# S5 parameter arithmetic on VectorE between the gates of the feed-forward layers, with its transfers queued one at a time

## The chip, the cores and the metric

The kernel runs on one core of a Trainium2 chip. The metric is device microseconds (us) of one execution, as a median of several. TensorE (PE in the profile) multiplies matrices; VectorE (DVE), ScalarE (ACT) and GpSimd (POOL) do elementwise work, each working off its own queue in order. SyncE (SP), ScalarE and GpSimd also issue transfers (DMA), and such an issue stands in the queue of the engine that makes it.

## The reference

One step of a two-layer model of width 1024, for a prompt of 256 tokens and 8 single-token samples (264 columns). Each layer is feed-forward, mixer, feed-forward, each followed by a residual sum and a layer norm. Layer 0 has the even mixer (attention and RWKV-7), layer 1 the odd one (S5). What matters here is the feed-forward and the parameters of S5, which depend on no token:

```
f  = (silu(x @ wg) * (x @ wu)) @ wd               # 1024 -> 2816 -> 1024
x  = layer_norm(alpha * x + 0.5 * f, g, b)

dt  = exp(log_dt)
ar, ai = exp(lr * dt) * cos(li * dt), exp(lr * dt) * sin(li * dt)
cr, ci = ((ar - 1, ai) divided by (lr, li))       # complex
bb  = (cr, ci) * (br, bi)                         # complex, per group, state and channel
s_t = (ar, ai) * s_(t-1) + bb @ u_t               # scan over the tokens
y   = c_re @ sr - c_im @ si + d_skip * u
```

## The kernel before, in words

Tokens lie along the columns, channels on the 128 partitions. Each weight block of 128x128 is loaded in float32, in chunks of 8 blocks (512 KB) on SyncE's queue (`raw`, line 188), and split in two halves: ScalarE casts the high half (`wh`, line 197), VectorE subtracts (`wl`, line 198). A block then takes three matmuls of 264 columns (lines 295 to 297): high by high, high by low, low by high. `Stream.take` starts the splits of the three chunks behind the one in use; four chunks fit.

A feed-forward (`ffn`) has three parts. First the gate blocks m = 0 to 2 are formed from the raw residual sum before its norm is known (`raw`, 48 blocks), while the norm is worked out beside it. Then for m = 3 to 21 there is one gate each: 16 blocks (48 matmuls) into `pg` and `pu`, a Silu on ScalarE (line 458), the product `h` on VectorE (line 460), its high half `hh` on ScalarE (461) and its low half `hl` on VectorE (462). Last come 8 down-projections (`pd`, 22 blocks each), each followed by its part of the residual sum in `put_r`. `stats` ends it: VectorE makes `nmu` (line 389), centres block 0 (line 398) and takes the reciprocal (391); GpSimd centres blocks 1 to 7 in four instructions (line 398 too). VectorE then multiplies each block by `rstd` (line 409), ScalarE scales it (402), and both split it (`xh` 414, `xl` 415). I call the norm at the end of layer 0's mixer the first norm, and that at the end of layer 0's second feed-forward the second norm; the feed-forward behind each begins with raw products.

The S5 parameters are worked out beside the trunk by two Python generators. `s5_first` runs in the first feed-forward: exponentials and sines (on VectorE already), powers of the pole, the zero-order hold, eight readout pieces (a complex product of 64 columns and one of 256), whose results go through TensorE to DRAM (`kd`, `gxd`) 12 pieces later. `s5_second` runs in layer 0's second and layer 1's first feed-forward: powers of the rotation, four rotation tables (`rot`, written to `rotd`), eight products into `FT` (lines 1527 to 1532), and eight pieces that finish the table `T` (1548 to 1551). Each `yield` ends a piece, and `advance` takes one, scheduled behind the last low half `hl`. All of the arithmetic through `tt` and `ts` is on GpSimd. The transfers of `s5_second` are on GpSimd's queue, behind a copy of the first norm's `rstd` (`anchor`).

The order of each engine's queue is set by a scheduler from the traced program; `issue_after` puts an instruction behind another.

Of the kernel before, what the change touches and what calls it, by code (L numbers as in the profile page):

```python
# [30 lines left out]
# pi / 2 and ln 2 in parts of few bits  # L31
# the set of activation tables that has Exp and Ln
# [4 lines left out]
G1 = 3  # L37
CW = 0.5 * math.exp(-0.5)

# blocks of the combined projection  # L40
# [5 lines left out]
# columns of the packed per-channel vectors  # L46
# [5 lines left out]
# columns of the packed constants  # L52
# [107 lines left out]
# accumulators  # L160
# [17 lines left out]
        # what the loads are queued behind  # L178
# [40 lines left out]
class Trunk:  # L219
    def __init__(self, ctx, tc, a, order):  # L220
# [15 lines left out]
        # the pole's fourth power: cosine, sine, magnitude  # L236
# [10 lines left out]
    def load(self):  # L247
        """the tokens, and the operands that are needed later"""
# [23 lines left out]
    def banks(self, **groups):  # L272
        """deals out the groups of accumulators: streams of work that run side by side have their own"""
        self.groups = {tag: list(g) for tag, g in groups.items()}
# [13 lines left out]
    def block(self, ps, key, xh, xl, start, stop, full=False):  # L288
        """three products of halves; the fourth is beneath float32's accuracy"""
# [10 lines left out]
    def behind(self):  # L300
        """what is traced within is queued behind the last block of the trunk's own work"""
# [5 lines left out]
    def advance(self):  # L307
        """a piece of what runs beside the trunk"""
# [4 lines left out]

    def new_r(self, ln, raw=True, tmp=None, pool=False):
        """with raw, the sum's halves are products' operands before its norm is known"""
# [14 lines left out]
    def put_r(self, ln, m, ps, base=None):  # L330
        """a block of the sum. The mean of the first two blocks is taken from all, so that the squares can be summed
        before the last block is there; it lies within two standard deviations of the mean"""
# [42 lines left out]
    def table(self, func, after):  # L375
        """has the table of a function loaded behind an instruction, before the function is needed"""
# [3 lines left out]
    def stats(self):  # L380
        """the norm of the sum"""
# [24 lines left out]
    def unit(self, k):  # L406
        """a block less the mean, over the standard deviation"""
# [18 lines left out]
    def fix(self, ps):  # L426
        """from a product with the raw sum: that with its norm, less a constant, and the constant"""
# [9 lines left out]

    def ffn(self, layer, f, ln_in, ln_out, raw=True):
        nc = self.nc
        with ExitStack() as ctx:  # L440
# [15 lines left out]
            def gate(m, pg, pu):  # L456
# [5 lines left out]
                self.last_v = nc.vector.tensor_tensor(out=hl[:, m, :], in0=h, in1=hh[:, m, :], op=ALU.subtract)  # L462
                return last
# [23 lines left out]
            for m in range(G1, KF):  # L487
# [6 lines left out]
                self.advance()  # L494
                if not raw_in and m < G1 + 5:
# [3 lines left out]
            for m in range(KD):  # L499
# [4 lines left out]
                self.advance()  # L504
# [16 lines left out]
    def slot(self, shape, name, dt=F32):  # L521
        """a tile of up to 4.2 KB a partition"""
        return self.rw.tile(shape, dt, tag="slot", name=name, bufs=11)

    def page(self, shape, name):
        """a tile of up to 2 KB a partition"""
        return self.rw.tile(shape, F32, tag="pg", name=name, bufs=5)

    def tmp(self, shape, name):
        """a tile of up to 1.1 KB a partition"""  # L530
        return self.rw.tile(shape, F32, tag="tmp", name=name, bufs=6)

    def in_proj(self, mb, ps, raw):
        """evacuates a block of the projection; for RWKV's with its token shift"""
# [27 lines left out]
    def _even(self, ctx, ln_in, ln_out):  # L562
# [4 lines left out]
        # small operands  # L567
        # each on its half of the rows
# [28 lines left out]
        # -1e30 where the key is not before the query  # L597
# [84 lines left out]
    def other_half(self, bone, sbb, idb, nmb):  # L682
        """the rest of the input projection, the attention and its half of the output projection, in pieces"""
# [31 lines left out]
    def samples(self, sbb, idx):  # L715
        """both mixers for the samples, in pieces"""
# [5 lines left out]
    def proj(self, mb):  # L722
        """a block of the projection, in pieces"""
# [9 lines left out]
    def load_exp_ln(self):  # L733
        """the table that has both functions"""
# [3 lines left out]
    def rwkv_first(self, lora, hv):  # L738
        """what takes tanh"""
# [18 lines left out]
    def rsqrt(self, o, x):  # L758
        """1 / sqrt(x) by exp and ln, and a step of Newton's; x is lost"""
# [8 lines left out]
    def rwkv_prep(self, hv, bone):  # L768
# [14 lines left out]
        for m in range(4):  # L783
            kr, lw, ti = self.kr_t[:, m, :], self.lw[:, m, :], self.ti[:, m, :]
            # unit key
# [9 lines left out]
            # decay, summed over a chunk  # L795
# [8 lines left out]
            # keys  # L804
# [18 lines left out]
    def rwkv_tokens(self, bone):  # L823
        """what takes the values"""
# [23 lines left out]
    def to_tokens(self, src, dst):  # L848
        """[(h2,j), m, t] to [(h2,t), (m,c), j], in pieces"""
        nc = self.nc  # L850
        d = dst.rearrange("p (m x) j -> p m x j", m=4)
        for m2 in range(2):
# [5 lines left out]
            # rows are (c2, t), columns (h2, j)  # L858
# [7 lines left out]
    def gram(self, x, out, banks):  # L866
        """[(h2,s), (m,c), (A|R) t] of x with A and R, masked, in pieces"""
# [14 lines left out]
    def rwkv_inverse(self):  # L882
# [5 lines left out]
        # inverse of I + L in ever larger diagonal blocks  # L888
# [42 lines left out]
    def rwkv_chain(self, bone):  # L931
        """from chunk to chunk"""
# [55 lines left out]
    def rwkv_gate(self):  # L988
        """gate and bonus with the group norm's factor and constant, in pieces"""
# [9 lines left out]
    def rwkv_out(self, c, bone):  # L999
        """group norm, bonus and gate of a chunk, the last with the samples"""  # L1000
# [14 lines left out]
        # 1 / sqrt by exp and ln, and a step of Newton's  # L1015
# [13 lines left out]
    def split_out(self, src, k0, s):  # L1029
        """the halves of a part of what goes into the output projection"""  # L1030
# [108 lines left out]
    def sample_values(self, idx):  # L1139
# [41 lines left out]
        # rows (g, d), columns (b4, h) to channels (h2, d), columns (m, b)  # L1181
# [5 lines left out]
    def sample_rwkv(self):  # L1187
# [10 lines left out]
        # partitions (half, b, h)  # L1198
# [44 lines left out]

    def complex(self, scr):
        """temporaries, and products of pairs of real and imaginary parts"""
        nc = self.nc
        Q = 32
        tt = nc.gpsimd.tensor_tensor
# [629 lines left out]
```

## Time and profile before

| | |
|---|---|
| three runs | 1212.99, 1215.94, 1216.66 us, median 1215.94 us |
| profiled execution | span 1214.5 us from its first to its last instruction; what lies around the span is not listed for it, and the median is 1.4 us above its span |
| TensorE | busy 1127.3 us, 93% of the span |
| VectorE | busy 848.4 us, 70% |
| ScalarE | busy 577.0 us, 48% |
| GpSimd | busy 451.1 us, 37% |

Busy shares are means over stages with different limits. Where TensorE runs without a pause, work on another engine costs nothing; the stretches where it stops, or runs at a lower granted clock, are those to look at.

### The profile page before, as it was taken

The numbers are of one execution on the slowest core, as the hardware profiler recorded it, in microseconds if no ns is written. First come the engines' busy times: TensorE is split into PE (matmuls) and PEld (weight loads), VectorE is DVE, ScalarE is ACT, GpSimd is POOL, SyncE is SP. The second block draws the span as 40 slices with busy tenths as digits, with TensorE's granted clock in tenths as the row PEclk, the third lists the DMA queues.
The fourth block names the chain that finished last, engine by engine and source line by source line (L and its number), as shares of the span: only waits on it lengthen the run. The fifth ranks groups of instructions, "written<-read, shape, count | busy, mean of one in ns | idle before, by whom it ended". The sixth has DMA issues, their size and how long they took to land.

```text
span 1214.5 us, 26118 instructions
## 1 busy us (share of the span) xinstructions
PE 1127.3 (93%) x10583; PEld 1067.4 (88%) x10583; DVE 848.4 (70%) x1364; ACT 577.0 (48%) x966; POOL 451.1 (37%) x731
## 2 busy tenths in 40 slices
PE   7999999889999998799999869999968999999995
PEld 7999899887986688799998769999957899999994
DVE  4966566989876679656579785555669699655564
ACT  4544544663355565444543354444352257544442
POOL 0399940446344207377799930000034201000001
PEclk9999999989999999899999879999978999999998
DMA  7666565534564334766666436665556253655551
GB/s 246 231 193 199 195 183 179 154 105 129 154 196 129 106 96 146 209 211 213 204 208 192 132 109 189 186 179 187 175 156 201 95 163 124 214 184 184 181 174 36
DMA packets 66122, 204.95 MB, mean 169 GB/s; under 512 B 13465, under 2 KB 16617, under 8 KB 65745
## 3 DMA queue, kind: packets, MB, share of 16 engines
q1 hardware_dynamic: 56400, 174.09, 45.5%
q0 software_dynamic: 6560, 23.27, 6.1%
q10 hardware_dynamic: 3040, 5.92, 1.5%
q8 instruction: 83, 1.36, 0.5%
q14 instruction: 39, 0.31, 0.1%
HBM read 192.22 MB, written 10.86 MB: 167 GB/s over the span
## 4 chain that ended last, share of the span: by engine, by line
PE 56%; POOL 21%; DVE 11%; DMA 6%; ACT 3%; issue 3%; ACTq 0%; SPq 0%; DVEq 0%; POOLq 0%
PE pd L295 5%; PE pd L297 5%; PE pd L296 5%; PE pg L295 4%; PE pg L296 4%; PE pg L297 4%; PE pu L296 3%; PE pu L295 3%; PE pu L297 3%; DVE wl L198 2%; PE pi L295 2%; POOL fv L1269 2%; POOL fu L1268 2%; POOL fu L1272 2%; POOL fv L1273 2%
## 5 line engine op out<-in xcount | busy, mean ns | idle before, releaser
L198 DVE TENSOR_TENSOR wl<-raw,wh 128x1024 fp32r<-128x1024 f32 (+2 forms) x317 | 405.3, 1279 | 213.8 <-ACT wh L197 212.9
L197 ACT CAST wh<-raw 128x1024 fp32r<-128x1024 f32 (+2 forms) x317 | 329.8, 1041 | 397.8 <-issue 173.8
L297 PE MATMUL pd<-hh,wl 128*128 128x264 f32 x704 | 201.1, 286 | 3.5 <-DVE wl L198 3.5
L295 PE MATMUL pd<-hh,wh 128*128 128x264 f32 x704 | 200.3, 285 | 0.0
L296 PE MATMUL pd<-hl,wh 128*128 128x264 f32 x704 | 199.2, 283 | 0.0
L295 PE MATMUL pg<-xh,wh 128*128 128x264 f32 x648 | 186.2, 287 | 6.5 <-ACT wh L197 2.3
L296 PE MATMUL pg<-xl,wh 128*128 128x264 f32 x648 | 184.9, 286 | 5.6 <-DVE xl L415 5.6
L297 PE MATMUL pg<-xh,wl 128*128 128x264 f32 x648 | 184.9, 285 | 0.0
L295 PE MATMUL pu<-xh,wh 128*128 128x264 f32 x608 | 172.6, 284 | 0.0
L296 PE MATMUL pu<-xl,wh 128*128 128x264 f32 x608 | 172.6, 284 | 0.0
L297 PE MATMUL pu<-xh,wl 128*128 128x264 f32 x608 | 172.4, 284 | 0.0
L297 PEld LDWEIGHTS pd<-hh,wl 128*128 128x128 f32 x704 | 132.6, 188 | 4.5 <-DVE wl L198 4.4
L295 PEld LDWEIGHTS pd<-hh,wh 128*128 128x128 f32 x704 | 132.4, 188 | 0.3
L296 PEld LDWEIGHTS pd<-hl,wh 128*128 128x128 f32 x704 | 132.4, 188 | 0.0
L295 PEld LDWEIGHTS pg<-xh,wh 128*128 128x128 f32 x648 | 123.3, 190 | 7.8 <-ACT wh L197 2.5
L296 PEld LDWEIGHTS pg<-xl,wh 128*128 128x128 f32 x648 | 123.5, 191 | 5.8 <-DVE xl L415 5.8
L297 PEld LDWEIGHTS pg<-xh,wl 128*128 128x128 f32 x648 | 122.9, 190 | 0.0
L398 POOL TENSOR_TENSOR r<-r,nmu 128x528 f32<-128x528 f32 (+1 forms) x24 | 31.0, 1320 | 240.8 <-DVE nmu L389 240.8
L296 PEld LDWEIGHTS pu<-xl,wh 128*128 128x128 f32 x608 | 114.9, 189 | 0.0
L295 PEld LDWEIGHTS pu<-xh,wh 128*128 128x128 f32 x608 | 114.7, 189 | 0.0
L297 PEld LDWEIGHTS pu<-xh,wl 128*128 128x128 f32 x608 | 114.3, 188 | 0.0
L1581 POOL MEMSET us<- 128x256 f32 x1 | 0.3, 312 | 177.5 <-PE pd L297 177.5
(509 smaller groups left out, 2423.5 us busy)
## 6 DMA issues: line engine op xcount, KB each, us to landing
raw<-in_w SPq DMA_DIRECT2D x308, 512.0 KB, 4.0
rotd<-T POOLq DMA_DIRECT2D x4, 768.0 KB, 5.5
raw<-in_w SPq DMA_DIRECT2D x7, 384.0 KB, 7.3
gxd<-gc SPq DMA_DIRECT2D x8, 256.0 KB, 2.5
qb<-qd POOLq DMA_DIRECT2D x8, 256.0 KB, 4.1
FT<-wd POOLq DMA_DIRECT2D x8, 256.0 KB, 9.9
bF<-in_bF POOLq DMA_DIRECT2D x8, 256.0 KB, 4.0
rot<-rotd ACTq DMA_DIRECT2D x5, 384.0 KB, 4.6
```

The costliest lines, as they stand in the source:

```text
L197: nc.scalar.copy(wh[:, :w], raw[:, :w])
L198: nc.vector.tensor_tensor(out=wl[:, :w], in0=raw[:, :w], in1=wh[:, :w], op=ALU.subtract)
L295: mm(ps, lhsT=wh, rhs=xh, start=start, stop=False)
L296: mm(ps, lhsT=wh, rhs=xl, start=False, stop=False)
L297: self.last_mm = mm(ps, lhsT=wl, rhs=xh, start=False, stop=stop)
L398: e.tensor_tensor(out=d, in0=d, in1=self.nmu[:, None, :].to_broadcast([128, k1 - k0, NT]), op=ALU.add)
L1268: tt(out=u, in0=x[0], in1=y[0], op=M)
L1269: tt(out=v, in0=x[1], in1=y[1], op=M)
L1272: tt(out=u, in0=x[0], in1=y[1] if im is None else im, op=M)
L1273: tt(out=v, in0=x[1], in1=y[0], op=M)
L1581: nc.gpsimd.memset(us[:, :, :, 0:8], 0.0)
```

## The change

The arithmetic of both generators moves from GpSimd to VectorE (`tt`, `ts`), and the three plain copies (`gx`, the magnitude of `rot`, `T`) to ScalarE. In the feed-forwards that begin with raw products only two gates of three take a piece, and the down-projections none; in the first feed-forward every gate takes one, and the down-projections the rest. `s5_second` no longer hangs its transfers on the first norm: `now()` makes GpSimd copy one column of the latest gate's `h` (`mark`) and puts the transfer behind that copy. `FT`'s eight loads, `bF`'s eight and `T`'s eight are issued one with a piece, `bF` one piece ahead of its use; every second rotation table has a tile of its own. The core of the diff:

```diff
                 self.last_v = nc.vector.tensor_tensor(out=hl[:, m, :], in0=h, in1=hh[:, m, :], op=ALU.subtract)
+                self.mark = h[:, 0:1]
...
                 last = gate(m, pg, pu)
-                self.advance()
-                if not raw_in and m < G1 + 5:
+                if not raw_in or m % 3:
                     self.advance()
...
                 self.last = self.put_r(ln_out, m, ps) + [self.last_mm]
-                self.advance()
+                if first:
+                    self.advance()
...
     def complex(self, scr):
-        tt = nc.gpsimd.tensor_tensor
+        tt = nc.vector.tensor_tensor
...
     def s5_first(self, scr):
-        tt = nc.gpsimd.tensor_tensor
-        ts = nc.gpsimd.tensor_scalar
+        tt = nc.vector.tensor_tensor
+        ts = nc.vector.tensor_scalar
...
-                nc.gpsimd.tensor_copy(gx[:, :, 0, :, 0], cG[:, :, 0])
+                nc.scalar.copy(gx[:, :, 0, :, 0], cG[:, :, 0])
...
     def s5_second(self, pool, scr):
-        tt = nc.gpsimd.tensor_tensor
+        tt = nc.vector.tensor_tensor
...
-        anchor = nc.gpsimd.tensor_copy(us[:, 0, 0], self.rstd[:, :Q])
-        with self.tc.issue_after(anchor.ins):
-            nc.gpsimd.dma_start(out=self.s0, in_=a["s5_in"])
-            nc.gpsimd.dma_start(out=self.as0, in_=self.as0d)
-            nc.gpsimd.dma_start(out=self.sel, in_=a["sel"])
-        for g in range(2):
-            for j in range(4):
-                src = wd[j, g].rearrange("q r p -> (q r p)")[None]
-                with self.tc.issue_after(anchor.ins):
-                    nc.gpsimd.dma_start(out=FT[g * 64 + j:g * 64 + 64:4].rearrange("p q r c -> p (q r c)"),
-                                        in_=src.to_broadcast([16, Q * 128]))
+        seen = scr.tile([128, 1], F32, name="seen")
+        @contextmanager
+        def now():
+            with self.tc.issue_after(nc.gpsimd.tensor_copy(seen, self.mark).ins):
+                yield
+        def loads():
+            for g in range(2):
+                for j in range(4):
+                    src = wd[j, g].rearrange("q r p -> (q r p)")[None]
+                    with now():
+                        nc.gpsimd.dma_start(out=FT[g * 64 + j:g * 64 + 64:4].rearrange("p q r c -> p (q r c)"),
+                                            in_=src.to_broadcast([16, Q * 128]))
+                    yield
...
-            with self.tc.issue_after(anchor.ins):
+            with now():
                 nc.gpsimd.memset(rot[:, :, 0, :, 0:1], 1.0)
                 nc.gpsimd.memset(rot[:, :, 1:3, :, 0:1], 0.0)
-                nc.gpsimd.tensor_copy(rot[:, :, 2, :, 1:64], q4(rho4).to_broadcast([128, SR // 4, 4, 63]))
+            nc.scalar.copy(rot[:, :, 2, :, 1:64], q4(rho4).to_broadcast([128, SR // 4, 4, 63]))
+            next(load)
...
                 if lv == 4:
                     yield
+                    next(load)
...
+        def factors(s):
+            bF = t_([128, SL, 2, 64], "bF", 2)
+            with now():
+                nc.gpsimd.dma_start(out=bF, in_=a["bF"][:, s * SL:s * SL + SL])
+            return bF
+        nc.gpsimd.memset(T, 0.0)
+        bFs = [factors(0)]
+        yield
         for s in range(Q // SL):
...
+            if s + 1 < Q // SL:
+                bFs.append(factors(s + 1))
+            bF = bFs.pop(0)
...
+            with now():
+                g, j = divmod(s, 4)
+                nc.gpsimd.dma_start(out=T[g * 64 + j:g * 64 + 64:4, :, j * 16:64],
+                                    in_=kd[:, g, :, 0:64 - j * 16].rearrange("q c f -> c q f"))
...
-            nc.gpsimd.tensor_copy(T[:, q], u)
+            nc.scalar.copy(T[:, q], u)
```

How this moves the queues is shown at three places. The first is GpSimd's queue (POOL) at the first norm. There L398 is the centring of blocks 1 to 7, and FT is the table that is loaded from `wd`. Before:

```order
L398 TENSOR_TENSOR r<-r,nmu 128x264
L398 TENSOR_TENSOR r<-r,nmu 128x528 x3
L1483 COPY us<-rstd 128x32
L1485 DMA s_6501<-in_s_in 128x512
L1486 DMA as_6502<-as0d 128x512
L1487 DMA sel<-in_sel 128x128
L1492 DMA FT<-wd 16x4096 x8
```

The same place in the changed kernel, where L1488 is the copy in `now()`:

```order
L398 TENSOR_TENSOR r<-r,nmu 128x264
L398 TENSOR_TENSOR r<-r,nmu 128x528 x3
L326 COPY rl<-gbl 128x8x2
L325 COPY rh<-gbh 128x8x2
L1488 COPY seen<-h 128x1
L1517 MEMSET T 128x2x4
L1518 MEMSET T 128x2x8
L1488 COPY seen<-h 128x1
L1496 DMA FT<-wd 16x4096
```

The eleven loads that stood straight behind the centring are gone from there; one load of `FT` stands behind each copy of a gate's `h`. The second place is GpSimd's queue at the second norm; L1548 to L1551 finish a slice of `T`. Before:

```order
L1548 TENSOR_TENSOR fu<-cst,dU 128x256
L1550 TENSOR_TENSOR fu<-fu,T 128x256
L1551 COPY T<-fu 128x256
L398 TENSOR_TENSOR r<-r,nmu 128x264
L398 TENSOR_TENSOR r<-r,nmu 128x528 x3
L326 COPY rl<-gbl 128x8x2
L325 COPY rh<-gbh 128x8x2
```

And in the changed kernel, at the same norm:

```order
L1488 COPY seen<-h 128x1
L1536 DMA bF<-in_bF 128x512
L1488 COPY seen<-h 128x1
L1550 DMA T<-kd 16x32x48
L398 TENSOR_TENSOR r<-r,nmu 128x264
L398 TENSOR_TENSOR r<-r,nmu 128x528 x3
L326 COPY rl<-gbl 128x8x2
L325 COPY rh<-gbh 128x8x2
```

No arithmetic of S5 is ahead of the centring any more; what is ahead of it hangs on a gate (`h`) of the feed-forward whose down-projections come in between. The third place is VectorE's queue (DVE) in the gates of the first feed-forward. Before, from one `h` to the next:

```order
L460 SCALAR_TENSOR_TENSOR h<-sg,pu 128x264
L198 TENSOR_TENSOR wl<-raw,wh 128x1024
L462 TENSOR_TENSOR hl<-h,hh 128x264
L198 TENSOR_TENSOR wl<-raw,wh 128x1024
L460 SCALAR_TENSOR_TENSOR h<-sg,pu 128x264
```

In the changed kernel, a part of a gate that carries a readout piece (`fu`, `fv` and `gx` are its temporaries and results):

```order
L462 TENSOR_TENSOR hl<-h,hh 128x264
L1269 TENSOR_TENSOR fu<-cb,ap 128x256
L1270 TENSOR_TENSOR fv<-cb,ap 128x256
L1416 TENSOR_SCALAR gx_969<-cb 128x4x16
L1271 TENSOR_TENSOR gx_968<-fu,fv 128x4x16x4
L1273 TENSOR_TENSOR fu<-cb,nai 128x256
L1274 TENSOR_TENSOR fv<-cb,ap 128x256
L198 TENSOR_TENSOR wl<-raw,wh 128x1024
L1275 TENSOR_TENSOR gx_968<-fu,fv 128x4x16x4
L460 SCALAR_TENSOR_TENSOR h<-sg,pu 128x264
L1269 TENSOR_TENSOR fu<-W,cb 128x64
L1270 TENSOR_TENSOR fv<-W,cb 128x64
```

Thirteen instructions of the piece now stand between the four of the gate. Over the whole program VectorE's queue grows by some 400 instructions, and GpSimd's shrinks by as many.

## Rows read from the trace of the kernel before

**Rows 1.** The page: span, busy share of each engine, granted clock in 40 slices.

```profile
span 1214.5 us, 26118 instructions
PE 1127.3 (93%) x10583; PEld 1067.4 (88%) x10583; DVE 848.4 (70%) x1364; ACT 577.0 (48%) x966; POOL 451.1 (37%) x731
PEclk9999999989999999899999879999978999999998
```

**Rows 2.** Windows: us, busy (x count) of PE, PEld, DVE, ACT, POOL; clock; DMA; GB/s.

```profile
25.00:50.00 25.00, 24.04 (x199) 23.83 (x198) 22.64 (x78) 14.11 (x23) 3.67 (x9) 1.00 0.71 246
...
212.00:236.00 24.00, 24.00 (x189) 23.61 (x188) 22.41 (x35) 15.29 (x28) 9.23 (x17) 1.00 0.58 177
...
484.00:508.00 24.00, 16.51 (x118) 16.12 (x118) 15.40 (x40) 12.82 (x24) 2.40 (x12) 0.86 0.69 185
...
508.00:608.00 100.00, 100.00 (x830) 100.00 (x830) 60.73 (x70) 48.73 (x72) 78.19 (x164) 1.00 0.67 215
...
644.00:672.00 28.00, 24.97 (x201) 24.33 (x199) 27.86 (x21) 10.00 (x13) 27.40 (x32) 1.00 0.65 200
672.00:724.00 52.00, 35.53 (x231) 33.60 (x231) 38.10 (x60) 23.06 (x37) 33.91 (x39) 0.80 0.37 115
```

**Rows 3.** Waits of TensorE: us in total, times, longest; 470 to 725, then 0 to 230.

```profile
PE raw L297 <- DVE wl L198: 8.9, 1, 8.9
PE pg L296 <- DVE xl L415: 5.6, 1, 5.6
...
PE pg L295 <- DVE fixc L430: 1.9, 1, 1.9
...
PE pk L1445 <- POOL gx L1274: 2.8, 1, 2.8
```

**Rows 4.** Timeline of VectorE and GpSimd at the second norm: start, us, instruction, [idle before].

```profile
685.16 0.42 DVE L389 TENSOR_TENSOR nmu<-nmu,dl 128x264 f32<-128x264 f32 x1
...
702.38 5.09 DVE L409 TENSOR_TENSOR r<-r,rstd 128x264 f32<-128x264 f32 x5 [11.43 <-POOL r L398]
...
701.61 4.88 POOL L398 TENSOR_TENSOR r<-r,nmu 128x264 f32<-128x264 f32 x4
```

**Rows 5.** Behind the first norm: GpSimd's and ScalarE's timeline, transfers of 476 to 496.

```profile
479.79 2.46 POOL L1492 DMA_DIRECT2D FT<-wd  x5
...
494.01 1.05 ACT L197 CAST wh<-raw 128x1024 fp32r<-128x1024 f32 x1 [6.03 <-DMA raw<-in_w]
...
raw<-in_w SPq DMA_DIRECT2D x4, 512.0 KB, 12.6
FT<-wd POOLq DMA_DIRECT2D x8, 256.0 KB, 9.9
```

**Rows 6.** Transfers of 625 to 700: line, count, KB each, median us to landing.

```profile
raw<-in_w SPq DMA_DIRECT2D x18, 512.0 KB, 4.2
bF<-in_bF POOLq DMA_DIRECT2D x6, 256.0 KB, 4.2
```

**Rows 7.** The splits on VectorE, 500 to 600 and 636 to 684: ns minimum/median/maximum.

```profile
L198 DVE TENSOR_TENSOR wl<-raw,wh x36: 1214/1225/1504, 501.0 to 598.4; 128x1024 fp32r<-128x1024 f32 x36
...
L198 DVE TENSOR_TENSOR wl<-raw,wh x14: 1410/1754/2878, 638.4 to 682.0; 128x1024 fp32r<-128x1024 f32 x14
```

**Rows 8.** VectorE's timeline in the first feed-forward, and one strided product by form.

```profile
48.86 0.22 DVE L1307 SCALAR_TENSOR_TENSOR er<-er,ex 128x64 f32<-128x64 f32 x1
49.00 0.43 DVE L462 TENSOR_TENSOR hl<-h,hh 128x264 fp32r<-128x264 f32 x1
49.34 0.22 DVE L1307 SCALAR_TENSOR_TENSOR er<-er,ex 128x64 f32<-128x64 f32 x1
...
57.33 0.23 DVE L1333 SCALAR_TENSOR_TENSOR fu<-fv,fu 128x64 f32<-128x64 f32 x1
57.59 0.23 DVE L1334 SCALAR_TENSOR_TENSOR fv<-fu 128x64 f32<-128x64 f32 x1
...
L1748 DVE TENSOR_TENSOR mix<-t,po x5: 610/617/631, 982.2 to 1004.2; 128x256 f32<-128x256 f32 x5
```

More of the change, by code (lines that the diff above doesn't have):

```diff
@@ L1501, in s5_second @@
         yield
+        load = loads()
         for s in range(Q // SR):
             q = slice(s * SR, s * SR + SR)
-            rot = T.rearrange("p q f -> p (q f)")[:, :SR * 192].rearrange("p (s r q c) -> p s r q c", s=SR // 4, r=3, q=4)
+            if s % 2:
+                rot = scr.tile([128, SR // 4, 3, 4, 64], F32, name="rot", tag="rot", bufs=1)
+            else:
+                rot = T.rearrange("p q f -> p (q f)")[:, :SR * 192].rearrange("p (s r q c) -> p s r q c", s=SR // 4, r=3, q=4)
             q4 = lambda v: v[:, q].rearrange("p (s q) -> p s q", q=4)[:, :, :, None]
-            with self.tc.issue_after(anchor.ins):
+            with now():
                 nc.gpsimd.memset(rot[:, :, 0, :, 0:1], 1.0)
                 nc.gpsimd.memset(rot[:, :, 1:3, :, 0:1], 0.0)
-                nc.gpsimd.tensor_copy(rot[:, :, 2, :, 1:64], q4(rho4).to_broadcast([128, SR // 4, 4, 63]))
+            nc.scalar.copy(rot[:, :, 2, :, 1:64], q4(rho4).to_broadcast([128, SR // 4, 4, 63]))
+            next(load)
             for lv in range(6):
@@ L1517, in s5_second @@
                     yield
+                    next(load)
             nc.gpsimd.dma_start(out=self.rotd[:, s * SR // 4:(s + 1) * SR // 4], in_=rot)
             yield
+        def factors(s):
[6 more added lines that the diff above has]
+        yield
         for s in range(Q // SL):
             q = slice(s * SL, s * SL + SL)
-            bF = t_([128, SL, 2, 64], "bF", 2)
-            with self.tc.issue_after(anchor.ins):
-                nc.gpsimd.dma_start(out=bF, in_=a["bF"][:, q])
+            if s + 1 < Q // SL:
+                bFs.append(factors(s + 1))
+            bF = bFs.pop(0)
             F0, F1, b0, b1 = FT[:, q, 0], FT[:, q, 1], bF[:, :, 0], bF[:, :, 1]
+            with now():
+                g, j = divmod(s, 4)
+                nc.gpsimd.dma_start(out=T[g * 64 + j:g * 64 + 64:4, :, j * 16:64],
+                                    in_=kd[:, g, :, 0:64 - j * 16].rearrange("q c f -> c q f"))
             u, v, x = (t_([128, SL, 64], n) for n in ("fu", "fv", "kt"))
@@ L1533, in s5_second @@
             yield
-        nc.gpsimd.memset(T, 0.0)
-        for g in range(2):
-            for j in range(4):
-                nc.gpsimd.dma_start(out=T[g * 64 + j:g * 64 + 64:4, :, j * 16:64],
-                                    in_=kd[:, g, :, 0:64 - j * 16].rearrange("q c f -> c q f"))
         dU = scr.tile([128, Q], F32, name="dU")
-        with self.tc.issue_after(anchor.ins):
+        with now():
             nc.gpsimd.dma_start(out=dU, in_=a["dU"])
+            nc.gpsimd.dma_start(out=self.s0, in_=a["s5_in"])
+            nc.gpsimd.dma_start(out=self.as0, in_=self.as0d)
+            nc.gpsimd.dma_start(out=self.sel, in_=a["sel"])
         dm = cst[:, C_DM:C_DM + 64]
```

## The prediction, made before the result was known

> **What bounds the kernel now.** I read the page first. TensorE is busy for 93% of the span, so only the stretches where it stops or runs slowly can give anything back; the granted clock is at its upper level in most slices and dips in a few [rows 1]. Windows of 25 us over the whole span, then the waits of TensorE, led to three such stretches that have S5's parameter work in them. The rest of the lost time (the end of the even mixer, the S5 mixer, the very end) has none of it and should stay.
>
> To price a stretch I count matmuls. In 508 to 608 TensorE never stops and starts 830 in 100 us, 0.1205 us each [rows 2].
>
> The worst stretch is the second norm. TensorE started 201 matmuls in 644 to 672 and 231 in 672 to 724 [rows 2], 432 in 80 us where 664 would fit. A norm costs some of that anyway: round the norm of the first feed-forward, where GpSimd has nothing of S5 left, 189 start in 24 us where 199 fit [rows 2], 10 short. That leaves 222 matmuls, 26.7 us. What made them late stands in two places. VectorE has `nmu` at 685.16, but GpSimd begins to centre with it only at 701.61, 16 us later, and VectorE sits idle for 11.43 us until a centred block is there [rows 4]; the splits `wl` that TensorE needs next are queued behind that, and TensorE waits 8.9 us in one piece [rows 3]. In those 16 us GpSimd worked off pieces of S5, the last slices of `T`, that are ahead of the centring in its queue. Its raw products (48 blocks, 144 matmuls, 17.3 us) had covered the norm until about 700, just not long enough. After the stop the clock is at the lower level (1.2 GHz) for a while: the mean over 672 to 724 is 0.80 [rows 2]. Before the norm VectorE is full, 27.86 of 28 us in 644 to 672, and the same split of 128x1024 takes 1754 ns by median against 1225 earlier [rows 2, 7], so that TensorE loses some of its time to late splits even ahead of the norm.
>
> The second stretch follows the first norm. Straight behind the centring GpSimd issues eleven loads, eight of them `FT`, at some 0.5 us each [rows 5]. The four weight chunks issued there take 12.6 us to land, against 4.2 later [rows 5, 6], so ScalarE waits 6.03 us for one [rows 5] with the Silu of the gate behind it, and through `h` and `xl` TensorE waits 5.6 us [rows 3]. In 484 to 508 it starts 118 matmuls where 199 fit: 81 short, 9.8 us, the clock at 0.86 in the mean [rows 2].
>
> The third is small: in the first feed-forward TensorE waits 2.8 us for a readout table `gx` of GpSimd [rows 3].
>
> **The change part by part.** *The centring.* Nothing of S5 that computes is ahead of L398 at the second norm now; the copies and transfers there hang on gates that lie eight down-projections back. So the centring can start at `nmu`, as at the first norm. Of the 26.7 us I keep 1.9, the wait of `pg` for `fixc` that the first norm shows too [rows 3], and 0.8 for the weights that the norm holds back: gain 24. VectorE's slow splits before it are in this sum.
>
> *The burst.* One load of 256 KB with a piece instead of eleven at once. Of 9.8 us the 1.9 for `fixc` stay: gain 7.9, less 0.4 for what the two ScalarE copies into `rot` cost that now stand inside the first norm, where ScalarE waits for VectorE anyway: 7.5. If that cover is gone they cost 2 times 0.5 us (504 columns, about half of a cast of 1024 at 1.05 [rows 5]).
>
> *The wait for `gx`.* The readout is done many gates before its use: gain 2.8.
>
> Sum of the gains: 34.3 us.
>
> *What VectorE pays.* This engine now does some 400 more instructions, and each weight split is queued among them. Prices by distance from start to start [rows 8]: 0.14 us for a narrow one between others, 0.26 for one that needs its forerunner, 0.34 at 264 columns; a product of 256 columns that writes with a stride takes 0.617 instead of some 0.42, 0.2 more. The `gx` products write and read with strides, but in runs of four, so I take the plain price and keep the other for the range. A gate without a piece: two splits at 1.2 and two at 0.34, 3.1 us, in TensorE's 48 x 0.1205 = 5.8. A readout piece adds 7 narrow and 6 wide: 1.0 + 2.0 = 3.0, so 6.1 in 5.8: VectorE falls behind by 0.3 at each of eight gates, 2.4. The pieces ahead of them (exponentials, sines, 52 narrow ones for the powers and the hold) fill five gates more; adding up VectorE's queue at these prices it is behind by 2 us there and by 5 at the worst gate. TensorE feels it only when the splits are late: three chunks of 24 matmuls are split ahead, 8.7 us, less a cast (1.05 [rows 5]) and a split (1.2 [rows 7]), leaves 6.4. So it just fits; I charge 2.5 us. The bounds: nothing, or all narrow ones at 0.26 and all wide ones 0.2 dearer. That is 52 x 0.12 + 8 x (7 x 0.12 + 6 x 0.2) = 6.2 + 16.3 = 22.5 more; 27 behind, less 6.4: 21 us.
>
> In the other two feed-forwards a cycle of three gates (17.3 us) carries the two halves of a rotation table: 9.3 + (24 x 0.14 + 6 x 0.2, those of 128 columns, between the two prices) + 6 x 0.34 = 9.3 + 4.6 + 2.0 = 15.9. It fits, and the products (2.0) and `T` (1.4) do with more room. At the dear prices the cycle is 9.3 + 7.8 + 3.2 = 20.3, 3 over, 12 for four. I charge nothing.
>
> Copies on ScalarE are hidden: it is busy 48% [rows 1]. The new copies `seen` make GpSimd wait for a gate; behind them are only transfers and memsets with one piece's lead. `bF` lands 4.2 us after its issue [rows 6], plus a copy and 0.5 for the issue, about 5 to 6, and it is needed a gate later, at 5.8 plus the low half. So VectorE waits for it hardly, and at most 1 us in a gate.
>
> A rule of the Trainium skill speaks against this part. The row first: `bF` landed in 4.2 us while VectorE was full [rows 2, 6]. The page "SBUF — State Buffer", section "Who interferes with whom", says that a transfer issued from GpSimd is held up where VectorE runs in a mode that uses the port pair shared with GpSimd; it names copies and operations with a scalar, and not the product of two tensors. The new work is nearly all of the latter, so by that rule, too, the transfers should not be late, and the sum is the same; if they were, the second rival below is the result.
>
> Sum: 1214.5 - 34.3 + 2.5 = 1182.7 for the span, and 1.4 more for what the median has above the span: **1184 us**.
>
> **The rivals.** *VectorE is the bound in the first feed-forward.* The strides or the chains are dear there. For: in the sum it is within 1.4 us of its cover already, and a readout gate is over TensorE's time. Against: in 25 to 50 the exponentials fill it to 22.64 of 25 us and TensorE still runs 24.04 [rows 2]. From half of the 16 to all but a little of the 21 us it gives 1184 + 8 to 18 = 1192 to 1202. A sentence of the skill points the same way: the page "Perfetto Trace Analysis", "Optimizing Scalar/DVE Operations", advises to move work off a full VectorE, where this change moves work onto it.
>
> *The stop behind the first norm stays, or the loads come late.* If weights are late there for their own sake (all eight raw blocks restart at once), or the loads now collide with them gate by gate, the 7.5 is not gained: 1192. At 9.9 us to landing, as `FT` had in the burst [rows 5], four of seven `bF` waits would be 4.7 us each, 19 us on VectorE, of which the cover takes 6.4 each time: no more than this.
>
> *Slower.* VectorE binds in both places: at the dear prices TensorE loses 21 in the first feed-forward and 12 in the next, 33 against gains of 34.3, so 1184 - 2.5 + 33 = 1215, no change. It ends slower only if the moved operations cost still more than that, beyond about 0.26 narrow and 0.54 wide; at 20% more on 150 such operations, 12 us more, 1227. Nothing in the rows is that dear.
>
> *The change does not do what it says* is out: the queues show it done.
>
> **How the numbers follow.** My forecast, both stops gone and VectorE within its cover, has 0.66, with a range of its own from 1178 (no charge, nothing left of the waits) to 1190. VectorE bound in the first feed-forward 0.17, the stop that stays 0.11, no change by dear prices 0.03, slower 0.03. The range reaches to the first two rivals: 1177 to 1202. About 0.3% (3.6 us) is what a measurement tells from no change here: faster 0.94, same 0.03, slower 0.03.
>
> **What would show it.** Right: at the second norm the first L398 on GpSimd starts within 1 us or so of `nmu`, and the wait of VectorE for it shrinks from 11.43 to 2 or less; no wait of TensorE over 3 us between the first norm and the end of the second feed-forward behind it; weight chunks land in some 4 to 5 us throughout; the split takes about 1.2 us everywhere in that stretch; GpSimd's busy time falls to well under half of its 451 us [rows 1]. Wrong: waits of TensorE for `wl` in the first feed-forward, with VectorE busy without a gap there (the first rival), or a row where ScalarE waits for `raw` behind the first norm (the second). I would be wrong above all if a readout piece takes over 4 us on VectorE.

## The result, and the profile after

The changed kernel takes 1184.53 us (median of 4 runs, 1183.51 to 1187.69), the kernel before 1215.72 in the runs beside them: a ratio of 0.9747, with a 95% interval of 0.9724 to 0.9769. 1184 was forecast, in a range of 1177 to 1202.

The page of the changed kernel: span, busy time and share of the engines with their instructions, then busy tenths and granted clock in 40 slices.

```profile
span 1181.7 us, 26162 instructions
...
PE 1119.5 (95%) x10583; PEld 1060.8 (90%) x10583; DVE 893.2 (76%) x1763; ACT 583.3 (49%) x986; POOL 205.7 (17%) x340
...
POOL 0000000364535314110110112000045102000001
PEclk9999999989999999999999999999979999999998
```

Against [rows 1], GpSimd has lost 245 us and VectorE gained 45, so VectorE is busier in a faster kernel. The 45 is a balance. Added up by source line over both traces, the arithmetic of the two generators took GpSimd 250 us and VectorE 13 us before, and takes VectorE 117 us now: it costs some 2.4 times less there. VectorE's other instructions, the same ones in both kernels, fell from 838 to 796 us; x2_centre below shows why. The clock's dip behind the second norm (slices 23 and 24 of [rows 1]) is gone.

Windows of the changed kernel (columns as in [rows 2]): the start of the first feed-forward's pieces, the stretch behind the first norm, the second norm.

```profile
25.00:50.00 25.00, 24.25 (x200) 24.03 (x200) 22.25 (x76) 14.09 (x28) 2.66 (x5) 1.00 0.80 255
480.00:508.00 28.00, 26.10 (x215) 25.91 (x215) 25.42 (x68) 19.71 (x35) 1.39 (x7) 1.00 0.51 158
667.00:690.00 23.00, 21.86 (x178) 21.68 (x177) 22.22 (x43) 16.89 (x28) 6.44 (x6) 1.00 0.49 147
```

Behind the first norm 215 matmuls start in 28 us where 232 fit (at 0.1205 us each), against 118 of 199 in [rows 2]. Round the second norm 13 of 191 are missing. In the 80 us of 626 to 706, where 664 fit, 640 start, against 432 in the 80 us of before. TensorE's waits of 460 to 700 (us in total, times, longest) hold nothing of the 8.9 and 5.6 us of [rows 3]; the 1.9 for `fixc`, which I kept, is there:

```profile
PE raw L295 <- DVE r L341: 3.2, 1, 3.2
PE pg L295 <- DVE fixc L430: 1.9, 1, 1.9
PE pg L295 <- DVE fixt L432: 1.1, 1, 1.1
```

The first of these stands at the end of the even mixer. The timeline of VectorE and GpSimd at the second norm (start, us, instruction), which answers to [rows 4]:

```profile
666.75 0.42 DVE L389 TENSOR_TENSOR nmu<-nmu,dl 128x264 f32<-128x264 f32 x1
...
667.56 1.80 DVE L391 RECIPROCAL rstd<-rstd 128x264 f32<-128x264 f32 x1
669.39 0.57 DVE L409 TENSOR_TENSOR r<-r,rstd 128x264 f32<-128x264 f32 x1
...
667.62 5.79 POOL L398 TENSOR_TENSOR r<-r,nmu 128x264 f32<-128x264 f32 x4 [68.03 <-ACT rstd L388]
```

The centring starts 0.9 us after `nmu`, and VectorE is not kept waiting for it. The transfers of the weights over the whole kernel (count, KB each, median us to landing), against the 12.6 us of [rows 5]:

```profile
raw<-in_w SPq DMA_DIRECT2D x308, 512.0 KB, 3.7
```

**Where the time came from.** Whole times differ between chips (the kernel before took 1214.3, 1217.1 and 1222.6 us in the three groups of runs below), so I compare stages inside one profile. Their borders are the starts of VectorE's reciprocal (L391) at the norms: 685.96 at the second norm of before, 667.56 above. A ends with the first feed-forward, B with the even mixer (the "first norm"), C with the next feed-forward (the "second norm"), D with the feed-forward behind that. From the end of D to the last of the six norms it is 305.7 before and 305.6 after. Each stage time comes from one profiled execution.

| us | A | B | C | D | median | ratio to before |
|---|---|---|---|---|---|---|
| before | 217.8 | 257.5 | 210.7 | 210.4 | 1215.7 | |
| after | 218.7 | 254.8 | 194.1 | 196.1 | 1184.5 | 0.9747 (0.9724 to 0.9769) |
| x1_spread | 218.4 | 258.5 | 226.9 | 202.5 | 1225.4 | 1.0079 (1.0050 to 1.0108) |
| x2_centre | 218.3 | 258.0 | 209.8 | 203.9 | 1208.8 | 0.9947 (0.9930 to 0.9965) |
| x3_second_pool | 221.6 | 254.8 | 206.2 | 198.2 | 1201.3 | 0.9876 (0.9839 to 0.9913) |
| x5_noise | 219.7 | 254.3 | 195.2 | 196.2 | 1188.3 | 0.9790 (0.9751 to 0.9828) |
| x1b_spread | 220.7 | 257.2 | 197.8 | 231.8 | 1226.0 | 1.0074 (1.0057 to 1.0090) |
| x3b_second_pool | 219.8 | 256.4 | 201.1 | 200.5 | 1196.1 | 0.9825 (0.9808 to 0.9841) |
| x9_full | 219.5 | 254.7 | 196.4 | 202.0 | 1192.7 | 0.9807 (0.9785 to 0.9829) |
| x6_burst | 219.4 | 256.4 | 199.7 | 196.1 | 1190.9 | 0.9781 (0.9764 to 0.9797) |
| x3c_copies | 219.5 | 261.8 | 193.5 | 195.9 | 1190.6 | 0.9741 (0.9723 to 0.9759) |
| x4_first_pool | 214.3 | 257.4 | 193.9 | 195.9 | 1184.5 | 0.9695 (0.9676 to 0.9715) |
| x7_layout | 215.1 | 257.9 | 193.9 | 195.9 | 1188.4 | 0.9724 (0.9707 to 0.9742) |
| x8_pace | 219.4 | 263.6 | 195.6 | 196.0 | 1195.6 | 0.9781 (0.9757 to 0.9805) |

The change gives 16.6 us in C, 14.3 in D and 2.7 in B, and costs 0.9 in A.

### The profile page after: what moved, and what is told of

The parts are those of the page before. It is cut to its first block, busy times and chain, and to the rows that moved or that the text cites. A ratio compares the mean times of both kernels' runs of the same rounds, so it can differ in the third digit from the quotient of the medians.

```text
span 1181.7 us, 26162 instructions
## 1 busy us (share of the span) xinstructions
PE 1119.5 (95%) x10583; PEld 1060.8 (90%) x10583; DVE 893.2 (76%) x1763; ACT 583.3 (49%) x986; POOL 205.7 (17%) x340
## 4 chain that ended last, share of the span: by engine, by line
PE 65%; DVE 20%; DMA 5%; ACT 4%; issue 4%; POOL 1%; ACTq 0%; SPq 0%; DVEq 0%; POOLq 0%
PE pd L295 7%; PE pd L297 7%; PE pd L296 7%; DVE wl L198 6%; PE pg L295 4%; PE pg L296 4%; PE pg L297 4%; DMA raw<-in_w 4%; PE pu L296 4%; PE pu L295 4%; PE pu L297 4%; ACT wh L197 2%; PE pi L295 1%; PE pso L1169 1%; DVE r L409 1%
## 5 line engine op out<-in xcount | busy, mean ns | idle before, releaser
L198 DVE TENSOR_TENSOR wl<-raw,wh 128x1024 fp32r<-128x1024 f32 (+2 forms) x317 | 390.2, 1232 | 181.0 <-ACT wh L197 179.7
L398 POOL TENSOR_TENSOR r<-r,nmu 128x528 f32<-128x528 f32 (+1 forms) x24 | 33.3, 1418 | 310.3 <-DVE nmu L389 242.3
L461 ACT CAST hh<-h 128x264 fp32r<-128x264 f32 x79 | 32.2, 409 | 56.9 <-DVE h L460 56.8
```

What stands on the lines that cost most here:

```text
L198: nc.vector.tensor_tensor(out=wl[:, :w], in0=raw[:, :w], in1=wh[:, :w], op=ALU.subtract)
L398: e.tensor_tensor(out=d, in0=d, in1=self.nmu[:, None, :].to_broadcast([128, k1 - k0, NT]), op=ALU.add)
L461: self.last = [nc.scalar.copy(hh[:, m, :], h), self.last_mm]
```

## The experiments

**x1_spread**: the queueing of the transfers alone. The kernel before with the `s5_second` of after, arithmetic and copies on GpSimd.

```diff
+                self.mark = h[:, 0:1]
...
-        anchor = nc.gpsimd.tensor_copy(us[:, 0, 0], self.rstd[:, :Q])
...
+            with self.tc.issue_after(nc.gpsimd.tensor_copy(seen, self.mark).ins):
```

> The kernel before, with only the transfers of the second half of S5's parameter work queued as in the changed kernel (one load behind each gate, the three loads for the samples and the selector at the end); all arithmetic stays on GpSimd, the pace stays one piece with each gate and each down-projection. By the theory of places the stop behind the first norm goes and nothing else: 1215.7 - 7.5 = 1208 us, the wait of ScalarE for the raw weights there gone, the second norm as late as before (VectorE idle over 10 us for a centred block). If the weights were late there for their own sake, and not because eleven loads went out at once, the time stays at 1215.7.

Slower. The stop behind the first norm did go (191 matmuls started in 475 to 500, 145 before). But VectorE's waits of 450 to 800 have a new row:

```profile
DVE h L460 <- POOL seen L1488: 33.5, 6, 10.6
```

The copy `seen` reads a column of `h` to hold a transfer until the gate. Behind arithmetic in GpSimd's queue it is late, and `h` has two buffers, so VectorE may not write the next one. In the changed kernel, where GpSimd's queue holds no such arithmetic, VectorE waits for no mark.

**x2_centre**: the kernel before, the second norm's centring on VectorE.

```diff
+        e = nc.vector if second else nc.gpsimd
...
-            self.center(k0, k1, nc.gpsimd)
+            self.center(k0, k1, e)
```

> The kernel before, with the centring of blocks 1 to 7 at the second norm alone done by VectorE, so that it cannot stand behind S5's pieces in GpSimd's queue; it costs VectorE about 3 us there. My prediction put the whole loss round that norm, 24 us, down to the late centring: by it about 1215.7 - 24 + 3 = 1195 us. The rival: GpSimd's products of 256 columns slow VectorE's operations in the down-projections ahead of the norm (1754 against 1225 ns for a split), VectorE falls behind there, and of the 24 us some 10 are lost before the centring is due at all. Then this edit gives back only 14 - 3 = 11 us: 1205 us, with the split still at 1.7 us ahead of the norm. If the centring does not matter: 1216.

It gave 6.4 us in D and 0.9 in C: even less than the rival's 11. My cause of the 24 us was the smaller part of it. The rest shows in TensorE's waits for VectorE in the kernel before, of 602 to 686, which all lie ahead of the centring (`dk`, `acc` and `sq` are parts of the norm's sums):

```profile
PE pd L297 <- DVE wl L198: 3.5, 3, 2.0
PE dl L364 <- DVE dk L357: 3.3, 1, 3.3
PE dl L363 <- DVE acc L367: 1.4, 1, 1.4
```

VectorE's own operations show what makes it late. By shape, busy us, mean ns of one and idle before it, in the down-projections ahead of the second norm, first before (620 to 685; `r<-xn,pd` is the residual sum, `rl` its low half):

```profile
L198 DVE TENSOR_TENSOR wl<-raw,wh 128x1024 fp32r<-128x1024 f32 x19 | 34.3, 1821 | 4.1 <-ACT wh L197 4.1
L369 DVE TENSOR_TENSOR sq<-sq,sqk 128x264 f32<-128x264 f32 x6 | 8.8, 1463 | 0.0
L371 DVE SCALAR_TENSOR_TENSOR rl<-r,vec,rh 128x264 fp32r<-128x264 f32 x7 | 6.6, 944 | 0.0
...
L339 DVE SCALAR_TENSOR_TENSOR r<-xn,pd 128x264 f32<-128x264 f32 x7 | 2.9, 416 | 0.0
```

then after (602 to 667):

```profile
L198 DVE TENSOR_TENSOR wl<-raw,wh 128x1024 fp32r<-128x1024 f32 x23 | 28.1, 1225 | 16.9 <-ACT wh L197 16.6
L371 DVE SCALAR_TENSOR_TENSOR rl<-r,vec,rh 128x264 fp32r<-128x264 f32 x8 | 3.9, 490 | 0.7 <-ACT rh L344 0.6
L339 DVE SCALAR_TENSOR_TENSOR r<-xn,pd 128x264 f32<-128x264 f32 x8 | 3.4, 426 | 3.7 <-PE pd L297 3.7
...
L369 DVE TENSOR_TENSOR sq<-sq,sqk 128x264 f32<-128x264 f32 x6 | 2.6, 426 | 0.0
```

Beside GpSimd's products, the operations shown with two tensors in SBUF take 1.5 to 3.4 times as long by mean; the one that has an operand in PSUM (`pd`) does not change. VectorE is full, and late, before the centring is due.

**x5_noise** and **x9_full**: the changed kernel with products on GpSimd that nobody reads. The edit of the first is shown; the second has six behind each of the last four gates and eight behind each down-projection, the mark on `hl` (see x1b_spread) and the centring of x2_centre.

```diff
+                        for i in range(6):
+                            nc.gpsimd.tensor_tensor(out=self.nz[:, i % 2], in0=self.r[:, m, 0:256], in1=self.nz[:, 2], op=ALU.mult)
```

> The changed kernel, with 42 products of 128 x 256 added on GpSimd that write a scratch tile nobody reads: six behind each of the first seven down-projections ahead of the second norm, so that GpSimd is busy beside them as in the kernel before, but done when the centring is due. By the theory of places alone this costs nothing: 1184.5. By the rival (two engines with operands in SBUF slow each other) VectorE's split rises from 1.22 to about 1.75 us there and the operations on a block of the sum from 0.43 to 0.95, VectorE needs 9.8 us for a down-projection of 8.0, seven times 1.8 less a cover of 6.4: 6 us or more are lost, 1190 to 1195, before the norm and without a late centring.

> The changed kernel with GpSimd kept as busy as in the kernel before from the last gates to the second norm and beside it: six products of 128 x 256 behind each of the last four gates and eight behind each down-projection, on a scratch tile that nobody reads, and the centring of that norm on VectorE, so that GpSimd's queue holds nothing up (the copies for the transfers read hl). In x5_noise a lighter dose (GpSimd 80% busy over 50 us) filled VectorE to 24.9 of 25 us and cost TensorE under 2 us. By the theory that the late centring makes the loss, 1184.5 and 3 us for VectorE's centring: 1188. If GpSimd's products, by slowing VectorE, make up the larger part of the 24 us round the second norm: 12 us or more, 1197 to 1204, with splits of 1.7 us or more from 620 to 700 and TensorE waiting for wl, dk and xl.

x5_noise lost 1.0 us in C, where 6 or more were expected: VectorE is full there (24.90 of 25 us in 625 to 650), but TensorE runs through these 25 us without a pause. x9_full lost 2.3 in C and 5.9 in D. Its windows:

```profile
620.00:671.00 51.00, 51.00 (x413) 50.60 (x412) 50.03 (x53) 23.29 (x34) 51.00 (x46) 1.00 0.58 179
671.00:700.00 29.00, 22.84 (x172) 22.65 (x171) 29.00 (x50) 15.95 (x28) 16.33 (x18) 0.88 0.33 104
```

VectorE has no gap in 671 to 700, and TensorE starts 172 matmuls where 241 fit. So the slowing is real and costs time without GpSimd's late centring; but the sum, 8.2 us, of which VectorE's own centring is an estimated 3.7 (three operations of 1241 ns), is less than the 12 I asked for. No run has that centring without the products, so D's 5.9 is not divided between the two. The added products also slow less than S5's own did: a split takes 1600 ns by mean in 620 to 671, not 1821, `sq` 900, not 1463.

**x1b_spread**: x1_spread with the mark on `hl`, which has no second writer.

```diff
-                self.mark = h[:, 0:1]
+                self.mark = hl[:, m, 0:1].bitcast(F32)
```

> The run x1_spread again, with the copies that hold a transfer until its gate reading a column of hl, which is written once, instead of h, which has two buffers: in x1_spread VectorE waited 33.5 us in six pieces to write h, for such copies that stood behind arithmetic in GpSimd's queue. If that wait was all of its loss, the stop behind the first norm is gone and nothing takes its place: 1214.3 - 7.5 = 1207 us. If spreading the transfers does not pay beside GpSimd's arithmetic, 1214 or more.

C fell to 197.8, and D rose to 231.8: GpSimd, held at the gates by the marks, came still later to the centring. VectorE's wait and TensorE's:

```profile
DVE r L409 <- POOL r L398: 32.7, 1, 32.7
...
PE raw L297 <- DVE wl L198: 34.2, 1, 34.2
```

This is the late centring again, three times as long as in [rows 4]. GpSimd starts 70 of S5's tensor operations beside the down-projections here, 69 in the kernel before; but the splits are slow for the last 32 us only (1896 ns by mean in 643 to 675, 1428 in the 33 us before), and C is 3.7 above that of after.

**x3_second_pool**, **x3b_second_pool** and **x3c_copies**: the changed kernel with the arithmetic of `s5_second` back on GpSimd; in the second the mark on `hl`, in the third the copies into `rot` and `T` on GpSimd too.

```diff
-        tt = nc.vector.tensor_tensor
+        tt = nc.gpsimd.tensor_tensor
...
-            nc.scalar.copy(T[:, q], u)
+            nc.gpsimd.tensor_copy(T[:, q], u)
```

> The changed kernel, with the tensor products of the second half of S5's parameter work back on GpSimd; pace (two gates of three, nothing with the down-projections), queueing of the transfers and the copies on ScalarE stay as changed. By the theory of places, and by the rival of slowed VectorE operations as well, the engine does not matter as long as nothing of it runs beside the down-projections or ahead of the centring: 1184 to 1188 us. If it is VectorE as the engine that brings the gain, 1200 us or more.

> The run x3_second_pool again with the same mending (the copies read hl instead of h; in x3_second_pool VectorE waited 8.9 us for them and TensorE stood still in 525 to 550). By both theories of the second norm, which say that it matters where and beside what the pieces run and not on which engine: 1184 to 1190 us. If VectorE as the engine is needed for the gain: 1197 or more.

> The run x3b_second_pool once more, with the copies into the rotation table and into T on GpSimd as in the kernel before, instead of on ScalarE. In x3b_second_pool these copies stood in ScalarE's queue ahead of the casts of the weights and waited for GpSimd's late arithmetic and transfers (12.9 us in one piece with 141 matmuls started in 525 to 550 where 209 fit, 6.5 us and several of 2 us behind 760), together some 12 us. If only the places matter, that is all that stood between it and the changed kernel: 1196.1 - 12 = 1184, between 1183 and 1188 us. If arithmetic on GpSimd still costs for its own sake, 1191 or more.

The first two fell short of the theory by 17 and 12 us, each for a queue of its own: VectorE waited 8.9 us for `seen`; then ScalarE's copy into `rot`, queued ahead of its casts, waited for the table's buffer:

```profile
538.06 0.61 ACT L1519 COPY T<-turn_m 128x504 f32<-128x504 f32 x1 [12.92 <-DMA rotd<-T]
```

With that mended, x3c_copies has the C and D of the changed kernel (193.5 and 195.9) with all of this arithmetic on GpSimd. VectorE is slowed there as well: beside gates, where it has room (`hl` 788 ns by mean in 700 to 800, not 426), and, against the expectation's "nothing of it runs beside the down-projections", beside those too. 51 of GpSimd's tensor operations start among the down-projections ahead of the second norm, the last at 652.0, 22.6 us before the centring at 674.6. TensorE does not stop, and VectorE comes out of it with room again:

```profile
628.00:652.00 24.00, 24.00 (x200) 24.00 (x199) 23.07 (x23) 11.74 (x17) 23.06 (x27) 1.00 0.72 220
652.00:676.00 24.00, 24.00 (x191) 23.61 (x190) 19.16 (x28) 11.24 (x16) 2.20 (x3) 1.00 0.68 208
```

Its whole time, 1190.6 us on the slowest of the chips, is 0.9741 of before; expected were 1183 to 1188 us.

**x6_burst**: the changed kernel with the loads at once again.

```diff
-                    with now():
...
+        anchor = nc.gpsimd.tensor_copy(seen, self.rstd[:, 0:1])
...
+                with self.tc.issue_after(anchor.ins):
```

> The changed kernel, with the eight loads of FT and the three for the samples and the selector issued at once behind the first norm, as before; everything else as changed. By my prediction the stop behind the first norm comes back: 1184.5 + 7.5 = 1192 us, raw weights landing in some 12 us there and ScalarE waiting about 6 us for one. If the burst was only harmful together with GpSimd's arithmetic: 1184.5.

C rose by 5.6 us, and D did not change. The transfers of 478 to 500 have the picture of [rows 5] again, with no arithmetic on GpSimd beside them:

```profile
raw<-in_w SPq DMA_DIRECT2D x4, 512.0 KB, 12.3
FT<-wd POOLq DMA_DIRECT2D x8, 256.0 KB, 9.9
```

The stop is back as it was (118 matmuls and a clock of 0.86 in [rows 2]):

```profile
484.00:508.00 24.00, 17.23 (x119) 16.84 (x119) 15.27 (x36) 13.34 (x24) 0.95 (x2) 0.86 0.71 185
```

80 matmuls short are 9.6 us, and without the 1.9 for `fixc` 7.7. C shows less than that, because the changed kernel loses a little elsewhere in C: it starts 193 matmuls in 556 to 580 and 190 in 604 to 628, x6_burst 201 and 197 in the same windows. These 15 matmuls are 1.8 us; what causes them no run shows.

**x4_first_pool** and **x7_layout**: what VectorE pays in the first feed-forward.

```diff
-        tt = nc.vector.tensor_tensor
-        ts = nc.vector.tensor_scalar
+        tt = nc.gpsimd.tensor_tensor
+        ts = nc.gpsimd.tensor_scalar
```

```diff
-                pp = lambda t: t[:, :, q].rearrange("p k q -> p q k")[:, :, None, :].to_broadcast(sh)
...
+                pp = lambda r: apt[:, r, q][:, :, None, :].to_broadcast(sh)
```

> The changed kernel with the tensor arithmetic of the first half of S5's parameter work (powers, hold, readout, samples) back on GpSimd. My prediction: TensorE's waits for wl in the first feed-forward (2.9 us in the profile of the changed kernel) go, the wait for the readout table gx (2.8 us) comes back: 1184 to 1185 us, no difference that can be measured. If VectorE's load in the first feed-forward costs more than its waits show: 1180.

> The changed kernel with the powers of the pole laid out a second time so that the readout's products read them in runs of four elements next to each other, not 256 bytes apart (two copies on GpSimd, the negative written straight into that layout). If the distance makes those products dear (0.62 us each, against 0.42 of the sums beside them), four of them in each readout piece get 0.2 us cheaper, VectorE falls behind by 0.8 us less at each of eight gates, and the waits of TensorE for wl there (2.9 us) go: 1181 to 1183 us. If the operand that repeats each element four times makes them dear, they stay at 0.62 and the time at 1184.5.

Eight builds with the first half as in the changed kernel have A between 218.7 and 221.6; x4_first_pool has 214.3 and x7_layout 215.1. In x4_first_pool TensorE waits neither for `wl` nor for `gx`: the wait for `gx` went with the pace (one piece a gate from the start, so `pk` comes at 133.2, not 104.7), not with the engine. The readout's products in the changed kernel, 60 to 130, by shape:

```profile
L1273 DVE TENSOR_TENSOR fu<-cb,nai 128x256 f32<-128x256 f32 x8 | 5.0, 629 | 0.1
L1270 DVE TENSOR_TENSOR fv<-cb,ap 128x256 f32<-128x256 f32 x8 | 5.0, 622 | 0.0
...
L1271 DVE TENSOR_TENSOR gx<-fu,fv 128x256 f32<-128x256 f32 x8 | 3.3, 419 | 0.1
```

and in x7_layout:

```profile
L1273 DVE TENSOR_TENSOR fu<-cb,apt 128x256 f32<-128x256 f32 x8 | 3.4, 422 | 0.1
...
L1270 DVE TENSOR_TENSOR fv<-cb,apt 128x256 f32<-128x256 f32 x8 | 3.3, 417 | 0.0
```

It was the reads far apart that were dear (256 bytes from one element to the next in `ap`, 128 in `nai`, at the same price); the strided writes into `gx` and the operand that repeats each element cost nothing extra. The whole time doesn't show the gain: x7_layout's median is 1188.4 us where 1181 to 1183 were expected, and its ratio can't be told from that of after.

**x8_pace**: the changed kernel with a piece at every gate and down-projection.

```diff
-                if not raw_in or m % 3:
-                    self.advance()
+                self.advance()
...
-                if first:
-                    self.advance()
+                self.advance()
```

> The changed kernel with the pace of before: one piece of S5 with each gate and each down-projection (two with the first gates of the first feed-forward), arithmetic on VectorE, transfers queued as changed. By places and by slowed operations alike GpSimd holds nothing that could be late or slow VectorE, and VectorE has room in a down-projection (5.4 us busy in 8.0, and a piece of 2 to 3.3): 1184 to 1188 us. If the pace is what the change lives on: 1195 or more, with VectorE full ahead of the second norm and waits for wl and dk.

(The first feed-forward kept one piece a gate, against what the expectation says.) C and D are 195.6 and 196.0: the pace costs 1.5 us in C and nothing in D once the arithmetic is on VectorE. That the whole time is 1195.6, and not 1184 to 1188, comes mostly from B, 263.6, whose code is that of after. Some 6 us of it are one stop in the even mixer, which x3c_copies has too (B 261.8) and after has not. ScalarE sits idle there before a copy, for something that the profile doesn't show; in x3c_copies the row is

```profile
ACT VT L864 <- remote: 4.3, 1, 4.3
```

and the mean granted clock is 0.83 in 355 to 375. Both runs are of the third group, so of one chip.

## Why the prediction was right, and where it was not

**The second norm, 24 us.** With the burst's 5.6 taken out, C and D gave 30.9 - 5.6 = 25.3. The size was right; the step "What made them late stands in two places" was half the story. x2_centre got 6.4 us back by a timely centring, net of an estimated 3.7 that it cost VectorE: about 10. C's part of the 25.3, 16.6 - 5.6 = 11.0, can't be the late centring's: C ends at the reciprocal, 0.8 us after `nmu`, and x2_centre left it nearly as it was. There TensorE waits for VectorE, which GpSimd's products slow: I had counted the slow splits into the sum and named no cause for them. x9_full shows that such slowing costs time, but its weaker products cost 2.3 in C; that a stronger and longer slowing makes up the whole 11.0 is argued, not shown, and the 4 or so of D that are left are not assigned. The change takes both causes away together. That the sum held with only one of them named is in part luck.

The Trainium skill has the sentence that I passed over: the page "SBUF — State Buffer", section "Who interferes with whom", says that a VectorE instruction with two inputs in SBUF contends with a GpSimd instruction that reads SBUF, and one with at most one such input outside the two-port modes does not. The trace agrees: 426 to 1463 ns for `sq`, 426 and 416 for `r<-xn,pd`. I had weighed the same section for transfers only.

**The burst, 7.5 us.** Right in mechanism, and in size at the stop itself: 7.7 by x6_burst's window, 5.6 net over C.

**The wait for `gx`, 2.8 us, and VectorE's charge of 2.5.** The wait went; x4_first_pool shows that the pace did it, and not the engine. The charge was mis-sized: A of x4_first_pool against after gives 4.4 us. A readout piece costs about 7 x 0.14 + 4 x 0.54 + 2 x 0.35 = 3.8 us from start to start and not 3.0. I had taken the products to read in runs of four, as they write; the reads of `ap` and `nai` do not, and x7_layout, which mends them, gets 3.6 of the 4.4 back. It stayed just under the 4 us that I had named as the mark of a wrong forecast. So moving the first half to VectorE did not pay (A grew by 0.9 where I had forecast 0.3 less); the kernel gains by the second half's queues.

The Trainium skill's page "SBUF — State Buffer", section "Door 1: The DMA port swizzle (why `[64,N]` ≈ `[32,N]`)", has accesses pay that leave a line of 16 bytes each time; the rows agree for the reads (0.62 and 0.42 us).

**Nothing charged in the other two feed-forwards.** Held: C and D are the same within 0.6 us with that arithmetic on either engine (after, x3c_copies).

**The engine or the place.** With the transfers spread, C + D is 429.5 us on GpSimd at the old pace (x1b_spread), 389.5 on GpSimd at the new (x3c_copies), 391.6 on VectorE at the old (x8_pace) and 390.2 on VectorE at the new. Either the engine or the pace is enough. Both take S5's products out of GpSimd's queue ahead of the centring, and both leave VectorE undisturbed in the last 20 us before it; further ahead, 51 such operations beside the down-projections cost nothing in x3c_copies.

**What would show it.** No wait of TensorE over 1.9 us between the first norm and the end of the second feed-forward behind it, splits of 1.2 us by median, weights in 3.7 us over the whole kernel: as named. GpSimd's 205.7 us are 46% of 451, not "well under half". And one sign of being wrong came in small, that of the first rival: in the first feed-forward of the changed kernel TensorE waits 2.9 us for `wl`.

**Left open.** B gave 2.7 us that I had not forecast, and runs from 254.3 to 263.6 over builds that differ only elsewhere. Its two highest values have the stop described at x8_pace; of the 2.7, TensorE's wait for ScalarE's `t` (2.7 us before, 0.4 after) is the larger part. No run looked for the cause of either. The 2.7 nearly makes up for what the burst (1.9 less than forecast, net) and A (1.2 less) fell short, so that 1184 was met so closely is luck.

x4_first_pool beats both kernels: its interval, 0.9676 to 0.9715 of before, lies below that of after, though the two were not timed on one chip.

## What to carry to other kernels

Ask of an engine's queue not how busy it is but what stands ahead of the one instruction that others wait for; taking that away is worth the same whether by another engine or by another pace. Look for operations that take longer in one stage than in another: what another engine does beside them is a cost of its own. A helper that marks a point by reading a tile holds that tile's buffer, and a copy given to an idle engine holds that engine's queue: both are free only as long as what they wait for is on time.

## What the hardware showed that I had not expected

- VectorE beside GpSimd's products: operations of 128x264 with two tensors in SBUF go from 0.43 us to 1.46 (`sq`) and from 0.49 to 0.94 (`rl`), the split of 128x1024 from 1.22 to 1.82; with one operand in PSUM it is 0.43 and 0.42.
- A product of 128x256 that reads elements 128 or 256 bytes apart takes 0.62 us, in runs of four next to each other 0.42; a write in runs of four with a gap of one 0.42.
- Eleven loads of GpSimd's at once make weight chunks land in 12.3 us (x6_burst), where the changed kernel's median is 3.7, with no arithmetic on GpSimd beside them.
